# A decoder step with expert retrieval on one Trainium2 core: shorter LayerNorm, scores of two keys in a PSUM bank, and scores, half-products and gathers spread over the weight-building stage

## The chip, the core and the metric

The kernel runs on one core of one Trainium2 chip, as one program. The metric is the device time of one execution in microseconds (us), of which smaller is better. A profiled execution also gives a span, from the first to the last recorded instruction, and a trace of every instruction on the core's engines: PE is the matrix engine (PEld its weight loads), DVE is VectorE, ACT is ScalarE, POOL is GpSimd, SP is SyncE, whose queue here only issues DMAs. Chip memory is DRAM; SBUF and PSUM are the core's own memories, and matrix products land in PSUM, which has eight banks of 2 KB in each of 128 partitions.

## The reference

One layer of a decoder, applied to 512 prompt tokens and to 32 sampled tokens (8 sequences of 4), 1024 wide:

```
proj = x @ w_in + b_in                     # q, k, v, g, ca, cg, 512 wide each
o    = retention(rope(q), rope(k), v)      # 4 heads, chunks of 128
mix  = [silu(g) * head_norm(o), conformer_conv(ca, cg)] @ w_out
x1   = layer_norm(ALPHA * x + mix, ln1_g, ln1_b)
q    = (x1 @ w_query).reshape(T, 8, 256)   # PEER: two half queries a head
s1, s2 = q[..., :128] . sub_keys_1, q[..., 128:] . sub_keys_2
idx, sv = the 16 best of the 16 x 16 sums of the best 16 of each side
gate = softmax(sv)
ffn  = sum over 8 heads x 16 experts of gate * gelu(peer_u[idx] . x1) * peer_v[idx]
y    = layer_norm(ALPHA * x1 + ffn, ln2_g, ln2_b)
```

There are 128 x 128 experts; one expert's `peer_u` and `peer_v` rows are 1024 numbers each. The outputs are `y` for prompt and sample, and the retention states and convolution caches of both. All is float32.

## The kernel before, in words

**Two ways to the same experts.** For 288 of the 544 tokens the kernel fetches the chosen experts by indirect DMA. Such tokens are in three groups: x1_0 (the first 128 prompt tokens, 128 slots of one expert a token), "s" (32 sampled tokens, four heads' experts laid side by side over 128 partitions, so 32 slots) and "b" (128 prompt tokens, 128 slots). A slot is one `gather` step (lines 578 to 601): POOL issues a DMA of 128 rows of 8 KB (`in_uv_dram`, both halves of an expert) into a buffer `g`; DVE forms the dot product with the token's `x1` (L586); ACT applies Gelu (L594) and the gate (L595); DVE adds the weighted second half to `acc` (L600). Three buffers `g` go round; the x1_0 and b groups have one more for each fourth slot. For the last 256 prompt tokens (ND = 256) the kernel goes through all 16384 experts densely, by 128 "keys" e of 128 experts:

- **scores** (`scores_of`, L814 to L821): load 512 KB of `in_ut_dram` into a buffer `uv` (four go round, UV = 4), and multiply it in 8 products with `x1T` into a PSUM tile `sp` of 128 experts x 256 tokens. A float32 product stands in the trace as two records, so a key has 16.
- **Gelu** of the scores by ACT into the SBUF tensors Ga, Gb, Gc, Gd (44, 32, 20 and 32 keys, `EG` and `E0S`).
- **build** (L891 to L913): the gate weights of each token and expert are not gathered but made, as a product of two one-hot matrices, A (made by ACT, L898 and L900, from the first key numbers) and B (made by DVE, L902 and L906, from the second key numbers and the gates split in three bf16 parts). It goes eight tokens at a time (TB); each four tokens' products (12 bf16 matrix products, L911) fill a PSUM tile `mm`, of which two go round.
- **V products** (`v_products`, L955 to L959): a key's second halves, again 512 KB (`in_uv_dram`) in a buffer `uv`, are multiplied with the weighted Gelus of the two halves b of the tokens and added up in the four PSUM banks `pB`. A key has 4 products, 8 records.

**Order of the dense part.** After the input projections, retention and convolution (the front), query projections and the selection of experts on DVE (`retrieve`, L517) run beside the scores of Ga's keys (L865) and Gb's (L870), and beside the slots of x1_0. Then `first_keys` (L924) builds the weights of the first 96 keys for all 256 tokens; for each four tokens DVE multiplies them into Ga and Gb (L935) and into those keys of Gc that have their scores already, and copies them for the others (L937). At each twelfth token one key of Gc gets its scores (`s_stage`, L915: Gelu of the tokens done into W, of the others into Gc, L919 and L921, and a multiplication, L922). The last DVE instruction of `first_keys` is the **fence**: in the s group the dots from slot FREE = 12 on, and in the b group all, are ordered behind it (L591). Then `run` (L1013) alternates one step of `phases` (V products of each key; the build of the last 32 keys; their scores) with two steps of `fetched` (slots of s and b, and the LayerNorm and output of each group, `finish`, L603). At the end come LayerNorm and output of the dense tokens from the banks pB (L1014 to L1019).

**LayerNorm** (`layer_norm`, L448): statistics by `bn_stats` and `bn_aggr` on DVE; the reciprocal root by two POOL instructions (`rsqrt`, L182); a small DVE product; then ACT computes (x - mean) * root (L460), DVE multiplies by the gain (L461) and adds the bias (L462). It is called by `mix_norm` (L487) for the five tiles of x1, whose result PE transposes (L493); by `finish`; and at the end.

**What sets the order.** The program is written as one sequence. A scheduler then reorders instructions on each engine by its own estimate of times; `behind(a, b)` adds an ordering without data. On the chip every engine works through its own list in order, and waits on semaphores. Buffers (`tile_pool` with `bufs`) make a writer wait until the buffer's last readers are done.

Of the kernel before, what the change touches and what calls it, by code (L numbers as in the profile page):

```python
# [8 lines left out]
F32 = mybir.dt.float32  # L9
# [10 lines left out]
D = 1024  # L20
# [12 lines left out]
TB = 8  # L33
KX = 60
UV = 4
FREE = 12
EG = (32, 20, 44, 32)
E0S = (0, 32, 52, 96)

# [54 lines left out]
def tile_step(ctx: ExitStack, tc: tile.TileContext, a, o):  # L94
# [350 lines left out]
            nc.sync.dma_start(o[5][0, b, CK - 1 - SQ:], t[b * SQ:(b + 1) * SQ])  # L445
        behind(nc.sync.dma_start(o[5][0, :, 0:CK - 1 - SQ], a["cache_conv"][0, :, SQ:]), lastk)

    def layer_norm(t, n, g, b, src=None):  # L448

        st = gw.tile([128, 2, 6], F32, name="lst", bufs=3)  # L450
        mv = gw.tile([128, 2], F32, name="lmv", bufs=3)
        halves = [slice(q * 512, (q + 1) * 512) for q in range(2)]
        for q, c in enumerate(halves):
            V.bn_stats(st[:n, q], src[q][:n] if src else t[:n, c])
        V.bn_aggr(mv[:n], st[:n])
        rs = gw.tile([128, 2], F32, name="lrs", bufs=3)
        rsqrt(rs[:n, 0:1], mv[:n, 1:2])
        V.scalar_tensor_tensor(rs[:n, 1:2], mv[:n, 0:1], -1.0, rs[:n, 0:1], op0=OP.mult, op1=OP.mult)
        for q, c in enumerate(halves if src else [slice(0, D)]):
            S.activation(t[:n, c], src[q][:n] if src else t[:n, c], AF.Identity, bias=rs[:n, 1:2], scale=rs[:n, 0:1])  # L460
            V.tensor_mul(t[:n, c], t[:n, c], g[:n, c])  # L461
            steps["ln"] = V.tensor_add(t[:n, c], t[:n, c], b[:n, c])  # L462

    bv[0] = bc_row("b_v", a["b_in"][:, 1024:1536], 512, fe)

# [134 lines left out]
                V.scalar_tensor_tensor(acc, v, wgt, acc, op0=OP.mult, op1=OP.add)  # L600
            yield

    def finish(x1, f, n, dsts, t):  # L603

        for q in range(2):
            c = slice(q * 512, (q + 1) * 512)
            V.scalar_tensor_tensor(t[:n, c], x1[:n, c], ALPHA, f[q][:n], op0=OP.mult, op1=OP.add)
        layer_norm(t, n, ln2[0], ln2[1])
        for p0, p1, dst in dsts:
            nc.sync.dma_start(dst, t[p0:p1])  # L610

# [197 lines left out]
    def place(e):  # L809

        g = max(i for i in range(4) if E0S[i] <= e)
        return GW[g][:, e - E0S[g]]

    def scores_of(e):  # L814

        u = uvp.tile([128, D], F32, name="uv").rearrange("p (k e) -> p k e", k=8)
        nc.sync.dma_start(u, a["ut"][e])
        sp = pdn.tile([128, ND], F32, name="sp")
        for k in range(8):
            T.matmul(sp, u[:, k], x1T[:, k, NG2:], start=(k == 0), stop=(k == 7))  # L820
        return sp  # L821

    qs = rp.tile([128, 16, n], F32, name="qs")
    eg = rp.tile([128, 4, PH, TK], F32, name="eg")
# [37 lines left out]
                V.tensor_sub(gr, gr, gtT[:, q, cs])  # L862
    topk_of("b", NS, range(0, PH, 2))
    topk_of("s", 0, range(2))
    for e in range(E0S[2], E0S[3]):  # L865
        S.activation(place(e), scores_of(e), AF.Gelu)  # L866
    gbs = ExitStack()
    gb = gbs.enter_context(tc.tile_pool(name="gb", bufs=1, side="right", reuse_waits="tile"))
    GW[0] = gb.tile([128, EG[0], ND], F32, name="Gb")
    for e in range(EG[0]):  # L870
        S.activation(place(e), scores_of(e), AF.Gelu)
    for _ in gather0:
        pass
    left.close()
# [16 lines left out]
    def build(bt, e0, ne, nt):  # L891


        pt = None
        for t1 in range(0, ND, TB):
            off = bt.tile([128, TB, NK], BF, name="off", bufs=1)
            for t in range(TB):
                S.activation(off[:, t], row, AF.Abs, bias=e1T[:, t1 + t:t1 + t + 1])  # L898
            A = bt.tile([128, TB, NK], BF, name="A")
            S.activation(A, off, AF.Relu, bias=1.0, scale=-1.0)  # L900
            M = bt.tile([128, TB // 2, ne, 2], BF, name="M")
            V.tensor_tensor(M, iot[:, e0:e0 + ne].unsqueeze(1).to_broadcast([128, TB // 2, ne, 2]),  # L902
                            pairs_of(e2T, t1).to_broadcast([128, TB // 2, ne, 2]), op=OP.is_equal)
            B = bt.tile([128, 3, TB // 2, ne, 2], BF, name="B")
            for q in range(3):
                V.tensor_tensor(B[:, q], M, pairs_of(gtT[:, q], t1).to_broadcast([128, TB // 2, ne, 2]), op=OP.mult)  # L906
            for t in range(t1, t1 + TB):
                if t % nt == 0:
                    pt = pdn.tile([128, nt, ne], F32, name="mm")
                for q in range(3):  # L910
                    T.matmul(pt[:, t % nt], A[:, t - t1], B[:, q, (t - t1) // 2, :, t % 2], start=(q == 0), stop=(q == 2))  # L911
                if t % nt == nt - 1:
                    yield pt, slice(t - nt + 1, t + 1)  # L913

    def s_stage(e, n=ND):  # L915

        sp, G_ = scores_of(e), place(e)
# [4 lines left out]
        V.tensor_mul(G_[:, :n], G_[:, :n], W[:, :n])  # L922

    def first_keys():  # L924

        with tc.tile_pool(name="bt", bufs=2, reuse_waits="tile") as bt:
            done = 0
            for pt, ts in build(bt, 0, E0S[3], 4):
# [12 lines left out]
        return last  # L941

    def last_keys():

        with tc.tile_pool(name="bt", bufs=2, reuse_waits="tile") as bt:
            for pt, ts in build(bt, E0S[3], EG[3], 16):
                S.activation(GW[3][:, :, ts], pt.rearrange("p t e -> p e t"), AF.Copy)  # L947
                yield

    def v_row(e):  # L950
        vt = uvp.tile([128, D], F32, name="uv")
        nc.sync.dma_start(vt, a["uv"][e * NK:(e + 1) * NK, D:])
        return vt

    def v_products(e, vt, b):  # L955
        W = place(e)
        for q in range(2):
            T.matmul(pB[b][q], W[:, b * 128:(b + 1) * 128], vt[:, q * 512:(q + 1) * 512],  # L958
                     start=False, stop=(e == NK - 1), skip_group_check=True)  # L959

    def v_stage(e):
        vt = v_row(e)
# [103 lines left out]
```

## Time and profile before

| what | value |
|---|---|
| median of 3 runs | 1594.81 us (1591.84 to 1600.19) |
| profiled execution | 1605.06 us, of it the span 1603.2 us |
| mean granted TensorE clock | 0.968 |
| PE, PEld busy | 1499.9 us (94%), 1024.8 us (64%) |
| DVE, ACT, POOL busy | 1227.2 us (77%), 603.3 us (38%), 363.5 us (23%) |
| bytes moved by DMA | 503.77 MB, mean 314 GB/s |

The views used below: the windows view gives, for a stretch of the span, each engine's busy time with its count of records in brackets, then the granted clock of PE, the mean busy share of the 16 DMA engines and the GB/s. The chain of waits follows the work that ended last back in time. The timeline lists start, duration, engine, line, output and inputs, and in square brackets the idle time before an instruction and what ended it. The waits view sums the idle time of one engine and line by what ended it (us in total, times, the longest). The groups view lists busy time and mean ns of one.

In time the kernel has these stages: the front and x1 until about 480 us, query projections, selection and the scores of Ga and Gb until 862 us, `first_keys` from 862 to 994 us, V products with the gathers of s and b until 1588 us, and the last LayerNorm.

### The profile page before, as it was taken

What the parts mean: (1) busy time and instruction counts of PE and PEld (TensorE: products, weight loads), DVE (VectorE), ACT (ScalarE), POOL (GpSimd) and SP (SyncE); (2) the same over time, 40 slices, a digit from 0 to 9 for tenths busy, and PEclk for the clock granted to TensorE, in tenths of its full rate; (3) what the DMA queues carried; (4) which work ended last, traced back from release to release, by engine and by line L of the source; (5) the groups of instructions that cost most, each with busy time, mean ns of one, the idle gap of its engine ahead of it and who ended that gap; (6) DMA issues with size and microseconds to landing.
All of it is one profiled execution on the core that took longest, in us unless ns stands there. A gap on an engine that the chain in (4) does not pass through costs nothing. (4 is left out here: it accounts for less than half of the span.)

```text
span 1603.2 us, 21131 instructions
## 1 busy us (share of the span) xinstructions
PE 1499.9 (94%) x7174; PEld 1024.8 (64%) x7174; DVE 1227.2 (77%) x3158; ACT 603.3 (38%) x1686; POOL 363.5 (23%) x335
## 2 busy tenths in 40 slices
PE   7999999887899999999999997999999999999995
PEld 6878567455697667887888875444566655543332
DVE  4949988757668999999966689656877777766666
ACT  2325443145212233333624789413994111111111
POOL 1002224312331222222321000222223222222221
PEclk9999989988999999999999997999999999999998
DMA  9549677937668779998898321998999999999995
GB/s 363 224 166 370 248 259 263 365 127 275 218 261 359 258 281 339 358 340 328 324 390 336 112 92 62 388 397 333 387 362 384 424 424 423 424 424 423 424 424 211
DMA packets 99544, 503.77 MB, mean 314 GB/s; under 512 B 10183, under 2 KB 21191, under 8 KB 56549
## 3 DMA queue, kind: packets, MB, share of 16 engines
q0 software_dynamic: 42240, 305.12, 48.8%
q1 hardware_dynamic: 50749, 189.96, 31.1%
q10 hardware_dynamic: 6448, 7.36, 1.4%
q8 instruction: 56, 0.92, 0.2%
q14 instruction: 51, 0.42, 0.1%
HBM read 497.03 MB, written 5.80 MB: 314 GB/s over the span
## 5 line engine op out<-in xcount | busy, mean ns | idle before, releaser
L820 PE MATMUL sp<-x1T,uv 128*128 128x256 f32 x2048 | 466.1, 384 | 14.2 <-ACT Ga L866 8.3
L820 PEld LDWEIGHTS sp<-x1T,uv 128*128 128x128 f32 x2048 | 385.3, 191 | 88.7 <-issue 22.9
L600 DVE SCALAR_TENSOR_TENSOR acc<-g,wgt,acc 128x1024 f32<-128x1024 f32 x285 | 364.6, 1279 | 99.7 <-ACT wgt L595 98.2
L583 POOL DMA_INDIRECT g<-in_uv_dram,I x128 | 167.6, 1309 | 504.6 <-DVE acc L600 268.6
L594 ACT ACTIVATE act<-act 128x1 f32<-128x1 f32 x288 | 57.7, 200 | 591.8 <-DVE g L586 584.9
L586 DVE SCALAR_TENSOR_TENSOR g<-g,x1g 128x1024 f32<-128x1024 f32 x160 | 195.3, 1223 | 91.8 <-DMA g<-in_uv_dram,Ib 63.3
L583 POOL DMA_INDIRECT g<-in_uv_dram,Ib x128 | 135.7, 1060 | 487.7 <-DVE acc L600 313.5
L586 DVE SCALAR_TENSOR_TENSOR g<-g,x 128x1024 f32<-128x1024 f32 x128 | 154.5, 1214 | 26.3 <-DMA g<-in_uv_dram,I 26.1
L958 PE MATMUL pB<-uv,Ga 128*128 128x512 f32 x352 | 162.0, 603 | 0.5 <-issue 0.2
L898 ACT ACTIVATE off<-row,e1T 128x128 bf16<-128x128 bf16 x512 | 158.0, 388 | 1.1
L199 PE MATMUL mm<-x1T,w 128*128 128x384 f32 (+1 forms) x448 | 156.2, 503 | 0.2 <-issue 0.2
L199 PEld LDWEIGHTS mm<-x1T,w 128*128 128x128 f32 x448 | 85.4, 193 | 62.3 <-issue 32.1
L958 PE MATMUL pB<-uv,Gd 128*128 128x512 f32 x256 | 117.2, 601 | 2.0 <-DMA uv<-in_uv_dram 1.0
L958 PEld LDWEIGHTS pB<-uv,Ga 128*128 128x128 f32 x352 | 63.7, 189 | 82.9 <-issue 63.4
L958 PE MATMUL pB<-uv,Gb 128*128 128x512 f32 x256 | 114.6, 601 | 2.2 <-DMA uv<-in_uv_dram 1.8
L958 PEld LDWEIGHTS pB<-uv,Gd 128*128 128x128 f32 x256 | 46.1, 189 | 73.2 <-issue 71.3
L911 PEld LDWEIGHTS <-A 128*128 128x128 bf16 x1536 | 65.1, 100 | 37.1 <-issue 28.0
L958 PEld LDWEIGHTS pB<-uv,Gb 128*128 128x128 f32 x256 | 48.0, 192 | 57.2 <-issue 54.5
L911 PE MATMUL mm<-B,A 128*128 128x96 bf16 (+1 forms) x1536 | 69.4, 197 | 12.3 <-DVE Gc L937 9.8
L900 ACT ACTIVATE A<-off 128x1024 bf16<-128x1024 bf16 x64 | 67.4, 1053 | 23.6 <-PE mm L911 23.1
L958 PE MATMUL pB<-uv,Gc 128*128 128x512 f32 x160 | 72.3, 599 | 0.0
L906 DVE TENSOR_TENSOR B<-M,gtT 128x768 bf16<-128x768 bf16 (+1 forms) x192 | 69.4, 416 | 2.4 <-PE mm L911 2.3
(294 smaller groups left out, 1752.9 us busy)
## 6 DMA issues: line engine op xcount, KB each, us to landing
uv<-in_ut_dram SPq DMA_DIRECT2D x128, 512.0 KB
uv<-in_uv_dram SPq DMA_DIRECT2D x128, 512.0 KB
w<-in_w_in_dram SPq DMA_DIRECT2D x18, 1024.0 KB
w<-in_w_query_dram SPq DMA_DIRECT2D x15, 1024.0 KB
w<-in_w_out_dram SPq DMA_DIRECT2D x6, 1024.0 KB
g<-in_uv_dram,I POOLq DMA_INDIRECT x128
keys<-in_state_retention_dram ACTq DMA_DIRECT2D x4, 512.0 KB
out_dram<-keys SPq DMA_DIRECT2D x4, 512.0 KB
```

What stands on the lines that cost most here:

```text
L199: T.matmul(p[:, :n], w[m // 2][:, k, (m % 2) * 128:(m % 2 + 1) * 128], xT[:, k, c0:c0 + n], start=(k == 0), stop=(k == 7))
L583: G.indirect_dma_start(out=t, out_offset=None, in_=a["uv"], in_offset=bass.IndirectOffsetOnAxis(ap=idx[:, k:k + 1], axis=0))
L586: dot = V.scalar_tensor_tensor(t[:, :D], t[:, :D], 1.0, x1, op0=OP.mult, op1=OP.mult, accum_out=act[:, 0:1])
L594: S.activation(act[:, 1:2], act[:, 0:1], AF.Gelu)
L600: V.scalar_tensor_tensor(acc, v, wgt, acc, op0=OP.mult, op1=OP.add)
L820: T.matmul(sp, u[:, k], x1T[:, k, NG2:], start=(k == 0), stop=(k == 7))
L898: S.activation(off[:, t], row, AF.Abs, bias=e1T[:, t1 + t:t1 + t + 1])
L900: S.activation(A, off, AF.Relu, bias=1.0, scale=-1.0)
L906: V.tensor_tensor(B[:, q], M, pairs_of(gtT[:, q], t1).to_broadcast([128, TB // 2, ne, 2]), op=OP.mult)
L911: T.matmul(pt[:, t % nt], A[:, t - t1], B[:, q, (t - t1) // 2, :, t % 2], start=(q == 0), stop=(q == 2))
L958: T.matmul(pB[b][q], W[:, b * 128:(b + 1) * 128], vt[:, q * 512:(q + 1) * 512], start=False, stop=(e == NK - 1), skip_group_check=True)
```

## The change

Five things are changed.

1. **LayerNorm in two DVE steps.** (x - mean) * gain needs no root, so it is one `scalar_tensor_tensor` with the mean as its scalar; a second one multiplies by the root and adds the bias. The ACT pass and the small product go. With `table=True` (in `finish` of the b group and at the end) the root is ACT's Sqrt and a DVE reciprocal of 128x1 in place of the two POOL instructions.
2. **Two keys' scores a bank.** `sp` becomes a tile of 2 x 256 float32, a whole bank; for Ga's and Gb's keys two keys are computed into one tile, and one Gelu of 512 columns does both. There are two such tiles, as there were of the smaller ones.
3. **Scores of `first_keys` spread.** A key of Gc is due after tokens 8, 16, 28, 36, and so on, 24 times over the 256 tokens, instead of at each twelfth; and the first product of it is ordered behind the last product of the tokens' weights, where the scheduler had placed it freely.
4. **Four V halves in `first_keys`.** The last four of the 24 places load the V rows of keys 0 to 3 and multiply them for the tokens b = 0, also behind the tokens' products. The halves b = 1 come first in `phases`. The four rows keep the four `uv` buffers until then.
5. **The fence at slot 20.** FREE = 20 instead of 12.

```diff
-FREE = 12
+FREE = 20
...
-    def layer_norm(t, n, g, b, src=None):
+    def layer_norm(t, n, g, b, src=None, table=False):
...
-        rs = gw.tile([128, 2], F32, name="lrs", bufs=3)
-        rsqrt(rs[:n, 0:1], mv[:n, 1:2])
-        V.scalar_tensor_tensor(rs[:n, 1:2], mv[:n, 0:1], -1.0, rs[:n, 0:1], op0=OP.mult, op1=OP.mult)
-        for q, c in enumerate(halves if src else [slice(0, D)]):
-            S.activation(t[:n, c], src[q][:n] if src else t[:n, c], AF.Identity, bias=rs[:n, 1:2], scale=rs[:n, 0:1])
-            V.tensor_mul(t[:n, c], t[:n, c], g[:n, c])
-            steps["ln"] = V.tensor_add(t[:n, c], t[:n, c], b[:n, c])
+        rs = gw.tile([128, 1], F32, name="lrs", bufs=3)
+        if table:
+            S.activation(rs[:n], mv[:n, 1:2], AF.Sqrt, bias=eps_c[:n])
+        else:
+            rsqrt(rs[:n], mv[:n, 1:2])
+        cs = halves if src else [slice(0, D)]
+        for q, c in enumerate(cs):
+            V.scalar_tensor_tensor(t[:n, c], src[q][:n] if src else t[:n, c], mv[:n, 0:1], g[:n, c],
+                                   op0=OP.subtract, op1=OP.mult)
+        if table:
+            V.reciprocal(rs[:n], rs[:n])
+        for c in cs:
+            steps["ln"] = V.scalar_tensor_tensor(t[:n, c], t[:n, c], rs[:n], b[:n, c], op0=OP.mult, op1=OP.add)
...
-    def scores_of(e):
...
+    def scores_of(e, ne=1, after=None):
+
+        sp = pdn.tile([128, 2, ND], F32, name="sp")
+        for i in range(ne):
+            u = uvp.tile([128, D], F32, name="uv").rearrange("p (k e) -> p k e", k=8)
+            nc.sync.dma_start(u, a["ut"][e + i])
+            for k in range(8):
+                p = T.matmul(sp[:, i], u[:, k], x1T[:, k, NG2:], start=(k == 0), stop=(k == 7), skip_group_check=True)
+                if after is not None and i + k == 0:
+                    behind(p, after)
+        return sp[:, 0:ne] if ne > 1 else sp[:, 0]
...
-    for e in range(E0S[2], E0S[3]):
-        S.activation(place(e), scores_of(e), AF.Gelu)
+    for e in range(E0S[2], E0S[3], 2):
+        S.activation(place2(e), scores_of(e, 2), AF.Gelu)
...
-    for e in range(EG[0]):
-        S.activation(place(e), scores_of(e), AF.Gelu)
+    for e in range(0, EG[0], 2):
+        S.activation(place2(e), scores_of(e, 2), AF.Gelu)
...
-                if ts.stop % 12 == 0 and done < EG[1]:
-                    s_stage(E0S[1] + done, ts.stop)
+                if ts.stop != 4 * ((8 + 31 * (done + len(ahead)) // 3) // 4):
+                    continue
+                if done < EG[1]:
+                    s_stage(E0S[1] + done, ts.stop, mm)
                     done += 1
+                elif len(ahead) < UV:
+                    ahead.append(v_row(len(ahead)))
+                    behind(v_products(len(ahead) - 1, ahead[-1], 0), mm)
...
     def phases():
-        for e in range(EG[0]):
+        for e, vt in enumerate(ahead):
+            v_products(e, vt, 1)
+            yield
+        for e in range(len(ahead), EG[0]):
             v_stage(e)
             yield
...
-            finish(x1g, [ac[:, 0:512], ac[:, 512:]], w_, [(0, w_, dst)], t)
+            finish(x1g, [ac[:, 0:512], ac[:, 512:]], w_, [(0, w_, dst)], t, g == "b")
...
-        layer_norm(t, 128, ln2[0], ln2[1], pB[b])
+        layer_norm(t, 128, ln2[0], ln2[1], pB[b], True)
```

`place2(e)` is `place(e)` for the two keys e and e + 1; `mm` is the last product of the four tokens, which `build` now also yields; `v_products` returns its first product; `build` itself, the number of products and the bytes moved are as before.

More of the change, by code (lines that the diff above doesn't have):

```diff
@@ L601, in gather, with finish @@
             yield
-    def finish(x1, f, n, dsts, t):
+    def finish(x1, f, n, dsts, t, table=False):
         for q in range(2):
@@ L607, in finish @@
             V.scalar_tensor_tensor(t[:n, c], x1[:n, c], ALPHA, f[q][:n], op0=OP.mult, op1=OP.add)
-        layer_norm(t, n, ln2[0], ln2[1])
+        layer_norm(t, n, ln2[0], ln2[1], table=table)
         for p0, p1, dst in dsts:
@@ L812, in place, with place2 @@
         return GW[g][:, e - E0S[g]]
-    def scores_of(e):
[L816 to L821, printed above, removed]
+    def place2(e):
+        g = max(i for i in range(4) if E0S[i] <= e)
+        return GW[g][:, e - E0S[g]:e - E0S[g] + 2]
+    def scores_of(e, ne=1, after=None):
[8 more added lines that the diff above has]
+        return sp[:, 0:ne] if ne > 1 else sp[:, 0]
     qs = rp.tile([128, 16, n], F32, name="qs")
@@ L910, in build, with s_stage @@
                 for q in range(3):
-                    T.matmul(pt[:, t % nt], A[:, t - t1], B[:, q, (t - t1) // 2, :, t % 2], start=(q == 0), stop=(q == 2))
+                    mm = T.matmul(pt[:, t % nt], A[:, t - t1], B[:, q, (t - t1) // 2, :, t % 2], start=(q == 0),
+                                  stop=(q == 2))
                 if t % nt == nt - 1:
-                    yield pt, slice(t - nt + 1, t + 1)
-    def s_stage(e, n=ND):
-        sp, G_ = scores_of(e), place(e)
+                    yield pt, slice(t - nt + 1, t + 1), mm
+    def s_stage(e, n=ND, after=None):
+        sp, G_ = scores_of(e, 1, after), place(e)
         W = dw_.tile([128, ND], F32, name="W")
@@ L922, in s_stage, with v_row, v_products @@
         V.tensor_mul(G_[:, :n], G_[:, :n], W[:, :n])
+    ahead = []
+    def v_row(e):
+        vt = uvp.tile([128, D], F32, name="uv")
+        nc.sync.dma_start(vt, a["uv"][e * NK:(e + 1) * NK, D:])
+        return vt
+    def v_products(e, vt, b):
+        W = place(e)
+        for q in range(2):
+            p = T.matmul(pB[b][q], W[:, b * 128:(b + 1) * 128], vt[:, q * 512:(q + 1) * 512],
+                         start=False, stop=(e == NK - 1), skip_group_check=True)
+            first = p if q == 0 else first
+        return first
     def first_keys():
@@ L927, in first_keys @@
             done = 0
-            for pt, ts in build(bt, 0, E0S[3], 4):
+            for pt, ts, mm in build(bt, 0, E0S[3], 4):
                 for g, e0, e1, ready in ((0, 0, EG[0], True), (2, 0, EG[2], True), (1, 0, done, True), (1, done, EG[1], False)):
@@ L945, in last_keys @@
         with tc.tile_pool(name="bt", bufs=2, reuse_waits="tile") as bt:
-            for pt, ts in build(bt, E0S[3], EG[3], 16):
+            for pt, ts, _ in build(bt, E0S[3], EG[3], 16):
                 S.activation(GW[3][:, :, ts], pt.rearrange("p t e -> p e t"), AF.Copy)
                 yield
[L950 to L959, printed above, removed]
     def v_stage(e):
```

## Prediction

> **What bounds the kernel now.** I read first the windows view, stage by stage. The columns are busy us (records) of PE, PEld, DVE, ACT, POOL, then PE's clock, DMA share and GB/s.
>
> ```profile
> 560.00:580.00 20.00, 20.00 (x69) 12.05 (x68) 19.48 (x79) 6.77 (x16) 4.81 (x5) 1.00 0.65 221
> 840.00:862.00 22.00, 22.00 (x104) 19.36 (x103) 13.67 (x16) 4.76 (x17) 4.69 (x5) 1.00 1.01 416
> 862.00:902.00 40.00, 40.00 (x339) 35.52 (x337) 25.74 (x97) 28.20 (x82) 0.94 (x1) 1.00 0.49 182
> 902.00:994.00 92.00, 79.53 (x748) 66.47 (x746) 76.60 (x289) 80.25 (x220) 0.34 (x1) 0.88 0.21 70
> 976.00:984.00 8.00, 4.16 (x48) 3.79 (x48) 8.00 (x31) 7.87 (x22) 0.00 (x0) 0.50 0.00 1
> 1200.00:1580.00 380.00, 374.66 (x1166) 194.29 (x1165) 268.12 (x350) 75.47 (x273) 99.01 (x99) 1.00 1.01 418
> 1580.00:1588.00 8.00, 7.82 (x18) 2.96 (x16) 6.79 (x11) 0.50 (x2) 0.42 (x2) 1.00 0.03 10
> ```
>
> Four stages, four limits. Around 570 us DVE (selection and gathers) is full. Just before `first_keys` PE and the DMA engines are both full. In `first_keys` (862 to 994) DMA is nearly idle; its first 40 us are PE's alone, its end is DVE's and ACT's (8.00 and 7.87 of 8 us) while PE stands at half clock. In the V stage PE and DMA are full together until 1580, when the last bytes have landed.
>
> Which of the two sets the pace of the V stage is seen in the chain of waits (start, us, what) and in the waits:
>
> ```profile
> 1173.18 3.55 PE sp L820 x16
> 1176.73 3.43 PE pB L958 x8
> ...
> 1516.83 3.67 PE pB L958 x8
> ...
> 1577.05 10.79 PE pB L958 x24
> 1587.88 0.68 DVE lst L454
> ```
> ```profile
> SPq L952 <- PE pB L958: 400.6, 116, 30.8
> ```
>
> A key's V products take 3.43 us where rows lie ready (1176) and 3.67 beside the gathers. The row loads wait for PE to free a buffer (400.6 us), not the reverse: PE sets the pace, DMA takes 0.24 us a key from it.
>
> **The change, part by part.** The order listing of the changed kernel says what the scheduler made of it: on every engine the same work in the same stages, so each part is priced where it stands.
>
> *LayerNorm in the front.* The groups view shows one hole on PE that a LayerNorm makes; the timeline gives it:
>
> ```profile
> 430.84 0.21 DVE L455 BATCH_NORM_AGGREGATE lmv<-lst 128x2 f32<-128x12 f32 x1
> ...
> 432.60 0.58 POOL L185 TENSOR_TENSOR lrs<-lrs,mhalf 128x1 f32<-128x1 f32 x1
> ...
> 436.34 1.94 PE L493 MATMUL mm<-cst,keys 128*128 128x128 f32 x8 [6.49 <-DVE keys L462]
> ```
> ```profile
> L607 DVE SCALAR_TENSOR_TENSOR yt<-x1g,acc 32x512 f32<-32x512 f32 (+1 forms) x4 | 2.6, 682 | 0.1
> L454 DVE BATCH_NORM_STATS2 lst<-pB 128x6 f32<-128x512 f32 x4 | 2.5, 663 | 0.0
> ```
>
> The root is ready at 433.2. The new first step (two of 0.682, L607's kind and size) fits between 431.05 and then; the second gives the first half at 433.9, so PE goes on at about 434.1: **-2.2 us**. Bounds: 0 and the whole hole, -6.5. The other LayerNorms of the front leave PE no hole, so they give nothing; ACT's pass was never on the path.
>
> *Two keys a bank.* What can go are PE's waits for a Gelu in 480 to 862:
>
> ```profile
> PE sp L820 <- ACT Ga L866: 8.3, 8, 2.8
> PE sp L820 <- ACT Gb L871: 2.8, 1, 2.8
> ...
> DVE g L586 <- DMA g<-in_uv_dram,Is: 8.9, 9, 1.8
> ```
>
> The longest is 2.8 us, and two more keys (7 us) of room in PSUM cover that, so PE may end its scores up to 11.1 us sooner. But DVE's list puts twelve slots of the s group ahead of the first product of `first_keys`, in both kernels, and those dots wait for DMA (8.9 us). With the three keys that PE has gained, 3 x 0.52 MB are out of the way of gathers at 416 GB/s: 3.8 us; the build starts when the slower of the two is there. I take **-3.6 us**; bounds 0 (the gathers hold it) and -11.1 (all of it). That 38 wider Gelus stand for 76 saves only ACT, which is not the bound there.
>
> *`first_keys`.* The tokens' products, 20 scores and the V work are the same on PE (18 V records in it before, 16 now). What comes in new are eight slots of s, 13 to 20, now not behind the fence. In the new DVE order they stand among the first 18 tiles of four tokens, that is the first 72 tokens, which now take 862 to 902. Each costs one dot and one accumulation:
>
> ```profile
> L600 DVE SCALAR_TENSOR_TENSOR acc<-g,wgt,acc 128x1024 f32<-128x1024 f32 x285 | 364.6, 1279 | 99.7 <-ACT wgt L595 98.2
> L586 DVE SCALAR_TENSOR_TENSOR g<-g,x1g 128x1024 f32<-128x1024 f32 x160 | 195.3, 1223 | 91.8 <-DMA g<-in_uv_dram,Ib 63.3 <-DMA g<-in_uv_dram,Is 28.0
> ```
>
> 8 x (1.279 + 1.223) = 20.0 us. DVE was busy for 25.7 of those 40 us; now 45.8, so DVE bounds this part, and it lasts 5.8 us longer at least. The windows view of the score line alone (PE, PEld) has
>
> ```profile
> 862.00:902.00 40.00, 33.02 (x147) 26.80 (x145) 1.00 0.49 182
> ```
>
> 147 of the 320 score records there; the new order has seven keys, 112. The other 35 go to the second part, 2.2 keys of 3.55 = 7.8 us more; V work is the same. There PE was busy 79.5, ACT 80.3, DVE 76.6 of 92 us, but unevenly: at 976 it stood half idle. Even spreading lets 7.8 us of PE fit into the idle 12.5, and ACT's two Gelus a key move along. So I leave that part at 92, give 1.2 us for dots that come late, and take **+7 us** for the build. Bounds: no better than PE's own work (119.5 of the 132): -12; no worse than all 20.0 added: +20.
>
> *Start of the V stage.* Four rows half used are 4 x 1.72 = 6.9 us of work for PE, as long as the first new row needs at the free DMA; before it had 2 rows there. I take 0, bounds -1 and +4.
>
> *V stage.* Eight gathers fewer ride along, so eight keys run at 3.43, not 3.67: 8 x 0.24 = **-2 us**. Bounds: 0, and the whole DMA time of the bytes, 8 x 1.05 MB / 418 GB/s = -20.1.
>
> SP's list now has the output of s after 24 V loads, not 34, and that of b ahead of the last five loads, which then wait for it. The timeline shows how s went:
>
> ```profile
> 1079.22 1.28 DVE L600 SCALAR_TENSOR_TENSOR acc<-g,wgt,acc 128x1024 f32<-128x1024 f32 x1 [0.60 <-ACT wgt L595]
> ...
> 1095.62 0.42 SPq L610 DMA_DIRECT2D out_dram<-yt  x1
> ```
>
> From the fence at 994 twenty slots took 86 us beside the build of the last keys, and the output came 15.1 us after the last. Now it is twelve, 0.6 x 86 = 52, so the output some 67 us after the fence. The 24th load comes when 20 keys are through, at 3.67 each or more: 73 us. So SP should hardly stand; 0, and +5 if it does.
>
> *The end.* Rows of the timeline, and in brackets the idle time:
>
> ```profile
> 1583.35 1.29 DVE L600 SCALAR_TENSOR_TENSOR acc<-g,wgt,acc 128x1024 f32<-128x1024 f32 x1 [0.60 <-ACT wgt L595]
> ...
> 1591.75 1.22 DVE L462 TENSOR_TENSOR yt<-yt,lnb 128x1024 f32<-128x1024 f32 x1
> ...
> 1592.00 1.40 POOL L185 TENSOR_TENSOR lrs<-lrs,mhalf 128x1 f32<-128x1 f32 x1
> ...
> 1596.37 1.29 DVE L462 TENSOR_TENSOR g<-g,lnb 128x512 f32<-128x512 f32 x2
> ```
>
> PE ends at 1587.84 and DVE at 1597.66, 9.8 us behind, with the b group's LayerNorm (`yt`) in between, since its last slot came only at 1583. Eight slots fewer at 3.7 us bring that 30 us forward and out of the way. Of the dense LayerNorms the new list has, from the time that the last but one bank is final (0.9 us ahead of PE's end), 8 steps of 0.682, 2 `bn_stats` of 0.663 and 3 small ones of L455's 0.21: 7.4 us, so DVE ends 6.5 behind PE: **-3.3 us**. ACT's Sqrt (a 128x1 pass) runs beside the steps. Bounds 0 (b is late again) and -4.9 (half).
>
> The root's second POOL instruction took 0.58 us at 432.60 and 1.40 at 1592.00, under a DVE product of two SBUF tiles. [...]
>
> **The sum.** -2.2 - 3.6 + 7 + 0 - 2 + 0 - 3.3 = -4.1 us: a span of 1599.1, an execution of 1601.0. The profiled execution lay 10 us above the median of the runs, so I take the difference over: 1594.81 - 4.1 = **1590.7 us**.
>
> **The rivals.**
>
> *DMA is the true bound of the V stage.* For it: 418 GB/s and a share of 1.01 over 380 us, and PE ends 8 us after the last byte. Against it: SP's waits for PE, and PE busy 374.7 of 380. Then the eight gathers are worth 20.1 and not 2: 1590.7 - 18.1 = 1572.6.
>
> *VectorE's list holds the build* (the slower side). DVE works in order, so each of the eight dots stands for its gather, and each accumulation for ACT. If nothing of the 20.0 us is hidden, the build grows by 20 and not by 7: 1590.7 + 13 = 1603.7. It is slower by over 0.5% from a growth of 19 us. For it: DVE was the full engine at 976, where PE stood. Against it: the eight stand where DVE had 14 idle of 40 us. A late gather would add to that:
>
> ```profile
> POOL g L583 <- DVE B L906: 25.3, 9, 6.2
> ```
>
> In the V stage POOL began nine gathers late, 2.8 us each, after build's products on DVE. Eight such delays, all on the path, are 22 us, 1626 in all; with three buffers a gather has about two groups of eight tokens, some 9 us, so I give that little. [...]
>
> *The start does not move.* The s gathers hold the build's start, and the front's gain is lost in the selection, which DVE bounds: 1590.7 + 5.8 = 1596.5. For it: twelve slots ahead of the build at 416 GB/s; against it, three keys' bytes out of their way.
>
> **How the numbers follow.** Forecast 0.52, with a range of its own of 1582 to 1600 (build 0 to +13, start 0 to -8); DMA bound 0.16; VectorE's list 0.17; start unmoved 0.15. A measurement of this kernel can tell about 0.5% from no change, 8 us: the bounds are 1586.8 and 1602.8. Faster: the DMA case and about a third of the forecast's, 0.34. Slower: most of the VectorE case, 0.14. Within: 0.52. The range reaches to both outer cases, 1574 to 1604.
>
> **What would show it.** PE's idle time behind Ga and Gb under 3 us; `first_keys` starting some 4 us sooner against the end of the front, its first 72 tokens taking 45 us or more with DVE full, and its end without the stretch at half clock; V keys at 3.43 for the last 30 us, with DMA share well under 1; b's output over 20 us ahead of PE's end, and DVE's end 6 to 7 us behind PE's. Wrong would be: a build over 150 us, SP standing for an output ahead of V loads, V keys at 3.43 beside gathers, or a front that the scheduler's new order moves by more than 3 us.

## The result, and the profile after

Twenty runs each gave 1600.3 us after the change and 1594.96 us before: a ratio of 1.0032 (95% interval 1.0018 to 1.0047), so 2.9 to 7.5 us **slower** where 4.1 us faster was forecast. A second set of twelve runs of the changed kernel gave 1.0013 (0.9989 to 1.0036), which does not exclude no change. Together they put the change between nothing and +7 us: inside the stated range, on the other side of no change.

The two profiled executions say the opposite at first sight: the changed kernel's took 1595.02 us with a span of 1592.9, 10.3 us less than the span before. One execution is not the median: before's profile lay 10 us above its median, this one 5 below. So the spans are taken apart by stage, and the changed kernel has a second trace. The boundaries are read from the timeline: first score product, first DVE product of `first_keys`, the start of the last such product of token 72, the fence, the last V product, the last instruction. All are us.

| stage | before | after | after, second trace | forecast | measured change |
|---|---|---|---|---|---|
| to the first score | 519.1 | 506.1 | 514.6 | -2.2 (the hole) | -3.8 in the hole |
| first score to build | 343.6 | 340.8 | 341.5 | -3.6 | -2.8, -2.1 |
| build, first 72 tokens | 39.9 | 42.9 | 45.1 | +5.8 or more | +3.0, +5.2 |
| build, the rest | 91.0 | 98.6 | 98.5 | 0 | **+7.6, +7.5** |
| fence to last V product | 594.2 | 595.0 | 594.8 | -2 | +0.8, +0.6 |
| last V product to the end | 15.4 | 9.5 | 9.6 | -3.3 | -5.9, -5.8 |

The forecast's build is +7 in one sum, with 1.2 of it given for late dots. With the hole for the first row, the terms add up to -1.1 and +1.6 us. Most of the 13 us by which the first row differs is no work of the change. In before's trace PE waited once for the retention state, and this row has no counterpart in the first trace after:

```profile
PE mm L412 <- DMA keys<-in_state_retention_dram: 6.1, 1, 6.1
```

This wait comes and goes in both kernels: the second trace after has 4.7 us of it, and the kernel before with one ordering edge added (below) none.

The front's own term is the hole ahead of the transposes of x1, here in the timeline after:

```profile
418.96 0.21 DVE L456 BATCH_NORM_AGGREGATE lmv<-lst 128x2 f32<-128x12 f32 x1
419.21 1.41 DVE L464 SCALAR_TENSOR_TENSOR keys<-mm,lmv,lng 128x512 f32<-128x512 f32 x2
...
420.00 0.58 POOL L185 TENSOR_TENSOR lrs<-lrs,mhalf 128x1 f32<-128x1 f32 x1
420.62 1.42 DVE L469 SCALAR_TENSOR_TENSOR keys<-keys,lrs,lnb 128x512 f32<-128x512 f32 x2
421.52 1.73 PE L500 MATMUL mm<-cst,keys 128*128 128x128 f32 x7 [2.71 <-DVE keys L469]
```

6.49 became 2.71. The first step fits beside POOL's root, as forecast, and PE goes on 0.94 us after the root (the forecast had 0.9). The root itself came sooner, 1.4 us after the statistics in place of 2.1.

The windows view shows the build. Columns: the window and its length, busy us (records) of PE, PEld, DVE, ACT and POOL, PE's clock, DMA share, GB/s. First before, cut at the 72nd token, then after:

```profile
862.70:902.60 39.90, 39.90 (x338) 35.45 (x337) 26.14 (x100) 28.21 (x83) 0.71 (x1) 1.00 0.49 178
902.60:993.60 91.00, 78.53 (x744) 65.75 (x743) 75.60 (x285) 79.87 (x220) 0.00 (x0) 0.88 0.21 70
```

```profile
846.90:889.80 42.90, 35.24 (x308) 30.70 (x306) 42.87 (x127) 30.98 (x96) 8.15 (x8) 0.92 0.75 268
889.80:988.40 98.60, 84.87 (x765) 70.54 (x766) 76.06 (x275) 80.65 (x223) 1.77 (x2) 0.93 0.30 102
```

In the first part DVE is full (42.87 of 42.90), as forecast. The second part is the surprise: PE has 6.3 us more to do, and it still idles 13.7 us, DVE and ACT 18 to 23. No engine bounds it; they wait for each other. In the waits of the build, two rows stand that before were nil (DVE's) or 3.7 us (ACT's), beside one that was 9.8 (before, then after):

```profile
PE mm L911 <- DVE Gc L937: 9.8, 9, 2.0
ACT W L919 <- PE sp L820: 3.7, 2, 3.1
```

```profile
ACT W L935 <- PE sp L833: 21.0, 13, 5.1
DVE Gc L938 <- ACT W L935: 15.4, 7, 4.3
PE mm L926 <- DVE Gc L968: 12.0, 8, 2.6
PEld L926 <- ACT A L915: 11.7, 6, 2.7
```

DVE waits for ACT's Gelu of a key, ACT for that key's scores on PE, and PE for DVE to free a bank of the tokens' products. PE's weight loads also wait for the matrices A (11.7 us; 1.1 before), which ACT makes behind the same Gelu in its list. One turn of that, in the timeline:

```profile
942.81 1.10 PE L926 MATMUL mm<-B,A 128*128 128x96 bf16 x12 [2.57 <-DVE Gc L968]
943.71 4.95 PE L833 MATMUL sp<-x1T,uv 128*128 128x256 f32 x16
...
944.53 0.17 DVE L968 COPY Gc<-mm 128x16 f32<-128x16 f32 x1
...
948.70 0.31 ACT L935 ACTIVATE W<-sp 128x172 f32<-128x172 f32 x1 [4.29 <-PE sp L833]
...
949.05 0.34 DVE L938 TENSOR_TENSOR Gc<-Gc,W 128x172 f32<-128x172 f32 x1 [4.35 <-ACT W L935]
```

PE stood 2.57 us because DVE had not yet emptied a bank. Then its list has the key's scores, 4.95 us, behind the tokens' product. By 944.7 DVE has used up all that PE made; its next instruction in order needs the Gelu, so it stands 4.35 us, and ACT stands 4.29. Behind the scores PE makes the products of eight tokens (24 records, from 948.50) and comes at 949.53 to the next key's scores; for that Gelu DVE stands another 1.04 us, at 953.6. The engines take turns.

In the V stage, a row of the chain of waits and one of PE's timeline:

```profile
1518.52 3.67 PE pB L950 x8
```

```profile
1545.40 38.01 PE L950 MATMUL pB<-uv,Gd 128*128 128x512 f32 x88 [0.97 <-DMA uv<-in_uv_dram]
```

A key takes 3.67 beside gathers, and 38.01 / 11 = 3.46 behind the last one, for 38 us; before, transfers had lasted until 8 us from PE's end. The windows of the two stretches:

```profile
1200.00:1541.00 341.00, 336.51 (x1007) 176.09 (x1006) 239.89 (x306) 59.27 (x219) 94.26 (x90) 1.00 1.01 419
1549.00:1583.40 34.40, 34.40 (x81) 14.92 (x79) 7.67 (x13) 1.87 (x3) 0.00 (x0) 1.00 0.37 122
```

DMA is full to the last gather (share 1.01, 419 GB/s); behind it it falls to 0.37, and PE alone is the limit (34.40 of 34.40).

The end, DVE's timeline (the b group's output left at 1554.8, 29 us ahead of PE's end):

```profile
1581.73 0.70 DVE L455 BATCH_NORM_STATS2 lst<-pB 128x6 f32<-128x512 f32 x1 [0.16 <-PE pB L950]
...
1588.24 1.42 DVE L469 SCALAR_TENSOR_TENSOR g<-g,lrs,lnb 128x512 f32<-128x512 f32 x2
```

DVE ends at 1589.66, 6.3 us behind PE's 1583.4; 6.5 was forecast.

### The profile page after: what moved, and what is told of

It reads as the page before. It is cut to its first block, busy times and chain, and to the rows that moved or that the text cites. A ratio compares the mean times of both kernels' runs of the same rounds, so it can differ in the third digit from the quotient of the medians.

```text
span 1592.9 us, 21001 instructions
## 1 busy us (share of the span) xinstructions
PE 1495.8 (94%) x7174; PEld 1021.8 (64%) x7174; DVE 1224.5 (77%) x3143; ACT 589.3 (37%) x1636; POOL 369.9 (23%) x329
## 5 line engine op out<-in xcount | busy, mean ns | idle before, releaser
L833 PE MATMUL sp<-x1T,uv 128*128 128x256 f32 x2048 | 467.1, 385 | 11.1 <-ACT Ga L881 4.7
L590 POOL DMA_INDIRECT g<-in_uv_dram,Ib x128 | 140.1, 1094 | 451.6 <-DVE acc L607 290.1
```

The costliest lines, as they stand in the source:

```text
L590: G.indirect_dma_start(out=t, out_offset=None, in_=a["uv"], in_offset=bass.IndirectOffsetOnAxis(ap=idx[:, k:k + 1], axis=0))
L833: p = T.matmul(sp[:, i], u[:, k], x1T[:, k, NG2:], start=(k == 0), stop=(k == 7), skip_group_check=True)
```

## The experiments

Three theories were set against each other. **Theory 1, VectorE's list**: the eight slots of s cost 20 us of DVE in the build, and that is the growth (the slower rival of the prediction). **Theory 2, the ring**: what costs is the order of a key's scores behind the tokens' last product. **Theory 3, the held rows**: the four half used V rows delay the V stage. The table has all runs; ratios are to the kernel before, with 95% intervals, the stages are those of the table above (us, one trace each).

| kernel | ratio | build: first 72 | rest | whole | fence to last V | end |
|---|---|---|---|---|---|---|
| before | 1 | 39.9 | 91.0 | 130.9 | 594.2 | 15.4 |
| after | 1.0032 (1.0018-1.0047) | 42.9 | 98.6 | 141.5 | 595.0 | 9.5 |
| after, again | 1.0013 (0.9989-1.0036) | 45.1 | 98.5 | 143.6 | 594.8 | 9.6 |
| after, scores free | 0.9940 (0.9914-0.9965) | 45.2 | 87.8 | 133.0 | 594.3 | 9.5 |
| after, fence 12 | 1.0001 (0.9981-1.0021) | 36.2 | 100.6 | 136.8 | 594.3 | 15.1 |
| after, no V halves | 1.0035 (1.0010-1.0060) | 43.8 | 100.9 | 144.7 | 593.3 | 9.5 |
| after, each 12th token | 1.0085 (1.0053-1.0116) | 47.2 | 110.5 | 157.7 | 595.0 | 9.5 |
| before + order | 1.0079 (1.0047-1.0112) | 38.3 | 108.7 | 147.0 | 592.8 | 15.5 |
| before + LayerNorm + two keys | 0.9959 (0.9933-0.9984) | 39.6 | 92.6 | 132.2 | 593.6 | 12.8 |
| before + fence 20 | 1.0002 (0.9975-1.0029) | 45.3 | 89.5 | 134.8 | 596.9 | 11.8 |
| after, free, fence 12 | 0.9945 (0.9919-0.9971) | 38.4 | 90.8 | 129.2 | 591.0 | 14.7 |
| after, free, fence 16 | 0.9957 (0.9934-0.9979) | 43.1 | 89.3 | 132.5 | 594.6 | 9.5 |
| after, tied 8 tokens earlier | 0.9954 (0.9934-0.9974) | 40.8 | 89.9 | 130.7 | 594.0 | 9.5 |
| the same, fence 16 | **0.9918** (0.9889-0.9947) | 35.4 | 88.6 | **124.0** | 594.7 | 9.5 |

**Scores free.** The order is taken out of the changed kernel:

```diff
-                    s_stage(E0S[1] + done, ts.stop, mm)
+                    s_stage(E0S[1] + done, ts.stop)
```

> The changed kernel with the scores of first_keys placed freely by the scheduler again, no order behind the tokens' last product (the V halves keep theirs); spacing, fence and all else as changed. Theory 2, the ring: PE has the scores done before DVE and ACT want them, the second part of the build goes from 98.6 to 91 or less, the waits of DVE for ACT's Gelu (15.4 us at the Gc line) go under 5 us, and the time is 5 to 8 us below the changed kernel's. Theory 1, VectorE's list: nothing changes in the first part (DVE full, 43 us) and the second; the time is within 2 us.

The second part fell to 87.8, with no wait of DVE for a Gelu at Gc left, and the ratio to 0.9940: 9.6 us faster than before, 12 to 15 faster than the changed kernel by its two sets (5 to 8 were expected). One ordering edge held more than the whole loss.

```profile
848.80:894.00 45.20, 45.20 (x362) 40.03 (x361) 44.05 (x127) 31.66 (x100) 9.99 (x9) 1.00 0.89 333
894.00:981.80 87.80, 73.29 (x712) 60.29 (x711) 74.67 (x276) 79.30 (x218) 0.02 (x1) 0.86 0.22 75
```

With the scores free PE is full beside a DVE that is nearly so (45.20 and 44.05 of 45.20): it takes scores early, 362 records in place of 308, while DVE is at the slots.

**The order alone, on the kernel before.** The first product of the key's scores is put behind the tokens' last:

```diff
-                    s_stage(E0S[1] + done, ts.stop)
+                    s_stage(E0S[1] + done, ts.stop, mm)
```

> The kernel before with one thing changed: the first product of each key's scores in first_keys is ordered behind the last product of the tokens' weights (20 keys, at each twelfth token, fence at 12). Theory 2, the ring: the build, 130.9 us before, becomes 8 us longer or more (in the changed kernel this order cost 141.5 - 133.0 = 8.5, and at each twelfth token it should cost more: 157.7 there with the fence at 20); DVE's waits for ACT's Gelu of such a key, nil before, come to 15 us or more, and the time is 8 to 25 us above before's. If the order costs only together with the eight slots of s (theory 1), the build stays within 3 us of 130.9.

The build grew by 16.1, all in the second part, and the runs by 0.8%. Its waits, of which the kernel before has none in the first row and 3.7 us in the second:

```profile
DVE Gc L924 <- ACT W L921: 36.1, 11, 5.7
ACT W L921 <- PE sp L820: 29.9, 11, 5.1
...
PE mm L913 <- ACT A L902: 15.5, 6, 2.6
```

Here the turns are regular, one for each key, 13.4 us apart: PE stands 2.6 us (at 896.6, 910.0, 923.4 and 936.9), then ACT 1.8 and DVE 3.1. PE stood longer for ACT's matrices A (15.5 us) than for a bank that DVE frees (10.3). So the ring needs neither the slots nor the V halves.

**Tied eight tokens earlier.** The spread places stay, but the edge leads to the product two tiles back, so that DVE has two banks in hand while PE is at the scores:

```diff
+                mms.append(mm)
...
-                    s_stage(E0S[1] + done, ts.stop, mm)
+                    s_stage(E0S[1] + done, ts.stop, mms[max(0, len(mms) - 1 - 2)])
```

> The changed kernel with each key's scores tied to the last product of the tokens eight tokens (two tiles) earlier, so that the keys stay spread but PE has them done while DVE is still at the tokens before. Theory 2, the ring: the slack of two tiles opens it; DVE's waits for such a Gelu fall from 15.4 us to under 5, the build comes from 141.5 to 136 or less, the time is 5 to 10 us below the changed kernel's. If it is the spreading itself, PE's work beside ACT's, that is dear, the build stays at 140 or more and the time within 3 us.

The build came to 130.7, DVE's waits for such Gelus to 0.4 us in the whole span, the ratio to 0.9954. Spreading is not dear; it is the place within a turn that was. This also answers another reading of the run with free scores, that its second part was short because PE had done more of the scores before it. Here the second part has as many PE records as in the changed kernel (774 and 765) and is 8.7 us shorter:

```profile
890.30:980.20 89.90, 81.18 (x774) 67.01 (x774) 78.12 (x280) 80.63 (x225) 3.22 (x2) 0.97 0.34 116
```

**Fence back at 12**, in the changed kernel (`FREE = 20` to `FREE = 12`).

> The changed kernel with the fence back at slot 12, all else as changed. Its build stage (first product of first_keys to the fence) took 141.5 us, 42.9 for the first 72 tokens and 98.6 for the rest; before it was 130.9 (39.9 and 91.0). Theory 1, VectorE's list: the eight slots of s are what makes the build longer, so it comes back to 131 or less, all of the 10.5; behind it the last keys run beside gathers again (+3) and the b group is late again at the end (+6), so the time is 1 to 3 us below the changed kernel's. Theory 2, the ring: a key's scores are tied behind the tokens' last product, ACT's Gelu waits for them, DVE's product for ACT and the next tokens' products for DVE; then only the first part comes back (to 40) and the second stays at 96 or more, and the time is 3 to 7 us above the changed kernel's.

Only the first part came back (36.2), the second stayed at 100.6, so theory 1 does not explain it. The time came out a little below the changed kernel's, not above as theory 2 had it; by the traces 4.7 gained in the build and 5.6 lost at the end should cancel.

**Fence 20 alone, on the kernel before** (`FREE = 12` to `FREE = 20`).

> The kernel before with the fence at slot 20, nothing else. Theory 1, VectorE's list: eight slots are 20 us of DVE in the first 72 tokens; DVE had 14 idle of 40 there, so the build grows by 5 us or more (from 130.9), and the end gains 5 to 6 (b's LayerNorm out of the way): within 2 us of before. Theory 2, the ring: without the tied keys PE runs ahead of DVE and the slots cost less than 3 us in the build; the end gains 5 to 6, and the time is 3 to 6 us below before's.

Build +3.9, end -3.6, V stage +2.7, ratio 1.0002: nothing in sum. The +3.9 lies between the two expectations.

**Scores free and fence 12.**

> The changed kernel with the scores of first_keys placed freely and the fence back at slot 12. With the ring (fence 20 against 12) the eight slots cost 141.5 - 136.8 = 4.7 in the build. Theory 2: without the ring PE was full in the first 45 us of the build, beside a DVE at 44, so the slots cost 2 us or less in a build of 133; what is lost is the end (+5.6), and the time is 3 to 6 us above that with the fence at 20 and free scores. Theory 1: the build comes to 128 or less, and the time is equal within 2.

The build is 3.8 us shorter than with 20 slots, not 2 or less: here theory 2 was wrong, and the equal time is what theory 1 had. The slots cost about 4 us with the ring (4.7), without it (3.8) and in the kernel before (3.9). The runs are equal to those with 20, since the end gives 5.2 back.

**No V halves ahead** (`len(ahead) < UV` becomes `len(ahead) < 0`).

> The changed kernel without the four V halves in first_keys: the 20 scores keep their places (the last after token 212), V rows are loaded and multiplied from phases on, or where the scheduler puts them. Theory 3, the held rows: four half used rows keep the four buffers, the V stage starts late by a load, and taking them out gains 2 to 4 us between the fence and the 64th V record. Against it: the halves are work that PE needs to do anyway in its idle time, and without them the end of the build saves at most what PE idles; within 2 us, or up to 4 us slower if the V work moves behind the fence.

From the fence to the 64th V record it took 23.3 us, with the halves 23.4: theory 3 falls. (Before it was 24.0, so the start of the V stage, forecast at 0, held.) The build did not get shorter without them; the scheduler then put as many V records, 16, ahead of the fence by itself.

**Each twelfth token**, no V halves, order kept.

```diff
-                if ts.stop != 4 * ((8 + 31 * (done + len(ahead)) // 3) // 4):
+                if ts.stop % 12 != 0:
```

> The changed kernel with the 20 scores at each twelfth token as before and no V halves ahead; the scores still ordered behind the tokens' last product, fence at 20. Theory 2, the ring: the cost goes with the number of tied keys in a stretch, and there are as many as with the new places: the build stays at 139 or more. If it is the new places that cost (24 in place of 20, late ones without cover), the build comes to 135 or less and the time is 4 us or more below the changed kernel's.

157.7: with the order kept, the new places are better than the old by 13 us (144.7 without halves). The spreading was a gain, under an order that cost more.

**LayerNorm and two keys a bank, on the kernel before** (these two edits of the diff alone).

> The kernel before with the new LayerNorm and two keys a bank, nothing else of the change. Both theories: the hole ahead of the transposes of x1 goes from 6.5 to 2.7 us (-3.8), from the first score to the build 341 in place of 343.6 (-2.5), the build as before (131), and the end as before, since b's output is late again (15): 6 us below before's time. If the gain in the front is lost ahead of the build, 0 to -2.

Ratio 0.9959, 6.5 us faster: hole 2.7, first score to build 340.6, build 132.2. The end came to 12.8, not 15 as expected. Together the two edits are a gain; what each of them gives is not separated by this run.

**The changed kernel again.**

> The changed kernel itself once more, for a second trace of it: the terms read from the first one sum to 0 to -2 us against before, the medians differ by +5. Theory 2, the ring, with a price that varies between executions (PE falls to half clock after its waits): the build takes more than the 141.5 us of the first trace, 143 to 147, the other stages stay (hole 2.7, V stage 595, end 9.5). If the build is 141 to 142 again, the rest lies in the front's DMA waits, which vary by some us.

The build is 143.6, as expected, but the 2.2 us more lie in the first part, where DVE is full; the second part repeated (98.6 and 98.5), so the price of the ring did not vary. The time to the first score was 514.6, 8.5 us longer than in the first trace of the same kernel.

**Scores free, fence 16.**

> The changed kernel with free scores and the fence at slot 16, between the two that were run. From those two: build 129.2 with 12 slots and 133.0 with 20, so 131; from the fence to the last V product 591 and 594.3, so 593; the b group's last slot comes some 16 us ahead of PE's end, enough for its LayerNorm (8 us), so the end stays at 9.5 to 10: 2 to 3 us below the kernel with free scores and 20 slots, the fastest of all. If b's output is still in the way, the end is 12 or more, and the time equal.

The end stayed at 9.5 with 16 slots, as expected; the build did not gain (132.5), and the time is that of its neighbours.

**Tied eight tokens earlier, fence 16.** Both edits on the changed kernel.

> The changed kernel with each key's scores tied eight tokens earlier and the fence at slot 16. From the runs: build 130.7 with 20 slots, about 1 us less for each slot kept out of it (129.2 against 133.0 for eight, with free scores), so 129; from the fence to the last V product 594; the end 9.5 as with 16 slots and free scores. Theory 2: 1 to 3 us below the same kernel with 20 slots and 8 to 10 below before. If the slots cost nothing in the build once the ring is open, equal to it within 1.

1580.64 us against 1593.47 of the kernel before in the same set: 0.8% **faster** than before (8.4 to 17.7 us by the interval, 8 to 10 expected), and so the fastest of all by its median; by the intervals it is not clear of the other kernels with free or earlier scores. The build takes 124.0 (129 expected). The two windows of its build:

```profile
853.70:889.10 35.40, 33.08 (x304) 29.13 (x303) 34.21 (x113) 27.47 (x83) 4.69 (x5) 1.00 0.79 295
889.10:977.70 88.60, 79.70 (x771) 66.10 (x770) 74.69 (x277) 82.17 (x227) 0.00 (x0) 0.98 0.24 78
```

ACT is busy for 82.17 of 88.60 us in the second part, more than PE (79.70) and DVE (74.69): that part is now near ACT's limit.

## Why the prediction was wrong, point by point

**The step that failed** is the second part of the build: "Even spreading lets 7.8 us of PE fit into the idle 12.5, and ACT's two Gelus a key move along. So I leave that part at 92". It came out at 98.6 and 98.5. The sum of busy times allowed it; the order did not. The front of this document lists that the scores' first product is now ordered behind the tokens' last product, and the working gave that edge no price at all. It is worth 141.5 - 133.0 = 8.5 us by the traces, 16.1 in the kernel before, and taking it out alone turned the sign. The rival on the slower side named the wrong mechanism: VectorE's list costs 4 us, not 20. In the first part DVE's busy time grew by 16.7 us (26.14 to 42.87) and the part by 3.0, so most of a slot fits into DVE's idle time. That the time still lies inside the stated range is luck: the upper end of the range was set for that rival, not for the ring.

**The first 72 tokens** were forecast at 45.8 us, DVE full. They took 42.9 and 45.1, and 45.2 with the scores free. The cause was right. In size the first trace stays under the 45 us that was given as a floor; one of the eight accumulations (1.26 us) came only behind that part.

**The front** gave 3.8 in place of 2.2, in each of the eleven traces that have the new LayerNorm (2.71 to 2.73 us of hole, against 6.49 in the three others). The mechanism was right. About 0.7 more came from the root: before, POOL issued a gather between the statistics and the root (0.94 us at 431.31 in its timeline). The other 0.8 is that DVE began the last statistics 0.6 us ahead of PE's end there, not 0.3 behind it.

**Two keys a bank** gave 2.8 and 2.1 in place of 3.6, but not for the reason given. The windows from first score to build, before and after:

```profile
519.10:862.70 343.60, 330.61 (x1519) 271.08 (x1518) 310.91 (x1042) 121.28 (x329) 88.35 (x73) 0.99 0.90 332
```

```profile
506.10:846.90 340.80, 328.10 (x1526) 270.44 (x1525) 308.88 (x1041) 115.80 (x288) 89.28 (x71) 1.00 0.90 335
```

PE's idle time is the same, 13.0 and 12.7 us. The waits for a Gelu fell from 11.1 to 6.0 us in total (under 3 was the sign given), and other waits took their place; 2.5 us less of busy PE is what is left. By an estimate that is the clock: before's trace has 6.83 us at half clock there (from 760.02, PE busy for 6.06 of them, so some 3 us more than at full clock), after's has none. The kernel with fence 20 alone, without this edit, had 339.9 from first score to build. So no gain of two keys a bank is shown.

**The V stage** was forecast at -2 and measured +0.8. The predicted saving is there: the last 192 of the 1024 V records took 87.1 us in place of 89.5. But from the 192nd to the 448th, where the last keys are built, it was 160.2 in place of 158.0; there the b group's gathers and the last keys' token products now come sooner (another 1.3 us went between the 448th and the 832nd). The fence alone does this: in all traces this stretch took 156.1 to 158.0 us with the fence at 12 and 159.1 to 162.2 with it at 20. Which of the two it is has not been separated.

**DMA as the true bound** falls as a forecast of time. Beside gathers it does set the pace: a key with a gather moves 0.52 + 1.05 MB, and at 419 GB/s that is 3.75 us, near the 3.67 to 3.70 that a key takes. PE's weight loads do wait for rows there, before (1200 to 1570) and after (1200 to 1541), so the reading that rows wait for PE and "not the reverse" was half of it:

```profile
PEld pB L958 <- DMA uv<-in_uv_dram: 19.2, 36, 1.0
```

```profile
PEld pB L950 <- DMA uv<-in_uv_dram: 21.3, 40, 1.4
```

But without gathers PE needs 3.46, so eight gathers away are worth 2 us and not 20: both limits lie close together.

**SP** hardly stood, as forecast: 0.7 us for the output of s, which left at 1056.4, 68 us after the fence (67 forecast), and 2.0 us for that of b.

**The end** gave 5.9 in place of 3.3, as b's LayerNorm was out of the way. The forecast of DVE's end behind PE's was right (6.3, forecast 6.5); the term was taken from 9.8 us, though the span before ended 15.4 us behind PE. The fence alone brings it to 11.8, the new LayerNorm alone (with fence 12) to between 12.8 and 15.1, both to 9.5.

**The root beside a DVE product** came as the row before had it. In the s group's LayerNorm after:

```profile
1053.08 1.27 DVE L464 SCALAR_TENSOR_TENSOR yt<-yt,lmv,lng 32x1024 f32<-32x1024 f32 x1
1053.13 1.30 POOL L184 TENSOR_SCALAR lrs<-lmv 32x1 f32<-32x1 f32 x1 [8.63 <-DVE lmv L456]
...
1055.12 1.27 DVE L469 SCALAR_TENSOR_TENSOR yt<-yt,lrs,lnb 32x1024 f32<-32x1024 f32 x1 [0.77 <-POOL lrs L185]
```

POOL's small instruction took 1.30 us beside a DVE product of 1.27 us (0.22 in the kernel before, with no such product beside it), and DVE then stood 0.77; nothing hangs on that output.

**What stays open.** The terms of the two traces sum to -1.1 and +1.6, the runs say +2.9 to +7.5 in one set and -1.8 to +5.7 in the other. The 1 to 4 us between these sums and the first set are not found in any stage; the second set holds both sums. The time to the first score varies by itself between 504.1 and 514.6 us in the eleven traces that have the same front, so a few us can't be placed with one trace of each.

## What to carry to other kernels

Busy sums say whether work fits into a stage, but not whether the lists let it: when an edge puts a producer's instruction right behind the last work that its consumer can live on, and two buffers are all that lies between, the engines take turns. Price every added ordering edge by what the consumer still has in hand when the producer comes to that instruction; here moving the edge two tiles back was worth as much as removing it. And when medians differ by 0.3%, compare the stages of several traces, not two spans.

## What the runs showed of the hardware

PE's clock fell to half after short waits, 2.57 us in the turn shown above, in steps of about 3.4 us. The windows of that turn (after; columns as before), cut where the clock changed:

```profile
936.07:939.48 3.41, 3.41 (x26) 2.96 (x25) 2.79 (x11) 3.35 (x11) 0.00 (x0) 1.00 0.34 135
939.48:942.90 3.42, 0.85 (x20) 0.73 (x18) 3.14 (x13) 3.39 (x12) 0.00 (x0) 0.99 0.52 157
942.90:946.31 3.41, 3.41 (x18) 2.96 (x18) 1.19 (x5) 1.51 (x6) 0.00 (x0) 0.50 0.00 1
946.31:949.72 3.41, 3.41 (x36) 3.03 (x35) 0.67 (x3) 0.89 (x3) 0.00 (x0) 1.00 0.06 8
```

A stretch in which PE was busy for 0.85 of 3.42 us, a quarter, was followed by one at half clock, and that one, in which PE was full, by full clock again; the key's scores took 4.95 us in place of 3.68. With the scores free, at the end of the build (the second stretch is the first at half clock):

```profile
946.10:949.51 3.41, 1.59 (x33) 1.32 (x29) 3.41 (x16) 3.38 (x11) 0.00 (x0) 1.00 0.00 0
949.51:952.92 3.41, 1.68 (x23) 1.47 (x20) 3.41 (x14) 3.35 (x9) 0.00 (x0) 0.50 0.02 5
...
963.16:966.58 3.42, 3.42 (x25) 2.20 (x24) 3.12 (x10) 3.36 (x10) 0.00 (x0) 0.50 0.00 0
966.58:969.99 3.41, 2.81 (x41) 1.86 (x39) 3.41 (x13) 3.34 (x10) 0.00 (x0) 1.00 0.02 5
```

Here half clock followed a stretch with 1.59 of 3.41 us busy, and stayed until a stretch that was full. These are no thresholds: by its records in the changed kernel's trace PE was busy for 1.63 of 3.42 us at 854.15 and full clock followed, and for 2.51 of 3.41 at 72.50 and half clock followed; a half-clock stretch with 2.78 of 3.41 busy (at 983.86) was followed by full clock. Where ACT and DVE set the pace, as here (3.38 and 3.41 of 3.41), PE had time left even at half clock (busy for 1.68 of 3.41); in the ring it made the turns that it hit 1.3 us longer. In the fastest kernel the build's two parts have a mean clock of 1.00 and 0.98, against 0.92 and 0.93 in the changed one.
